# Weight halves of the plain products placed 64 bytes further on in SBUF, modulo 256

## The chip, the cores and the metric

The kernel runs on one core of a Trainium2 chip. The metric is the device time of one execution in microseconds, the median of several runs; lower is better. Beside it stands one profiled execution, from which all rows of the profile come.

## The reference

One transformer block over 512 tokens of width 1024, in fp32: a gated feed-forward, a mixer of two kinds of attention, a second gated feed-forward, and a last norm.

```python
def swiglu(h, w_gate, w_up, w_down):
    return (jax.nn.silu(h @ w_gate) * (h @ w_up)) @ w_down        # D_FF = 2816

    x = x + 0.5 * swiglu(rmsnorm(x, norm_ffn1), w_ffn1_gate, w_ffn1_up, w_ffn1_down)
    x = x + hybrid_mixer(rmsnorm(x, norm_mix), w_in, ..., w_out, rel_bias)
    x = x + 0.5 * swiglu(rmsnorm(x, norm_ffn2), w_ffn2_gate, w_ffn2_up, w_ffn2_down)
    return rmsnorm(x, norm_final)
```

The mixer projects h with w_in (2840 columns), runs eight heads of block attention and eight heads of compressed, selected and windowed attention with shared keys and values, and projects the result with w_out (1024 by 1024).

## The kernel before

Activations lie transposed: 128 features on the partitions, 512 tokens along the free dimension. TensorE (PE) multiplies a stationary operand, which a weight load (PEld in the profile) brings into the array, by a moving operand that streams through it. Each fp32 factor is kept as two fp32r halves, a rounded one (hi) and the rest (lo). `mm3` forms a product as three matmuls: hi by hi (L101), hi by lo (L102), lo by hi (L103). The loads of the next matmul's weights run beside the matmul before it.

There are two kinds of weight halves, each made by ScalarE (hi, a copy with rounding) and VectorE or, in parts of the mixer, GpSimd (lo, a subtraction) from a chunk that a DMA from SyncE's queue has brought:

- `whi`, `wlo`, from the pool `wp` (five buffers each), made by `halves` (L92, L94, L96). They serve the plain gate and up products (`pgu`; the first four of 22 blocks of 128 hidden features in each feed-forward, and there alone), the way down (`pd`, moving operand `h`), and in the mixer the projections (`pp`), the value projections (`pv`, where whi and wlo are the moving operand and `xo` the stationary one), the compression (`pc`) and the output projection (`pw<-o` and `pw<-kvn`). With `pd` of the last two hidden blocks of the second feed-forward, too, whi and wlo move.
- `sph`, `spl`, from the pool `sp` of each feed-forward (L236, L237). They serve the gate and up products of the other 18 hidden blocks, which `Ffn.pair` forms two blocks at a time by a scheme of seven products of half the size (256 columns): `pu`, `pv`, `pw` from moving operands `xo` (B11 and the like) and `th`, `tl` (sums of blocks). These are called two-block products below. (The mixer has tiles of the names pv and pw of its own; their moving operand tells them apart: two-block `pv` and `pw` have `sph` or `spl` as the weights.)

The order is written out by hand. In each feed-forward `lay` makes a list of steps: a plain stage (four hidden blocks of gate and up, then their way down, whose matmuls follow one another), then two-block steps, between which `mixed` and `between` lay the way down of the four hidden blocks before: each such triple of matmuls (one `mm3` of `pd`, 512 columns) stands alone or with another between groups of two-block products of 256 columns. `go` calls loads, sums and halves a fixed number of steps ahead. In the mixer `run` mixes projection matmuls into the attention steps.

A pool lays its tiles out in the order in which their names are first asked for, and the pools follow one another. The program holds two tiles that nothing uses, and that only move what follows: `gap` (64 bytes, in `sp` behind th and tl) and `rest` (192 bytes, in `cp`). The first bytes of the operands of TensorE, along a partition, as the program before places them:

| tile | role on TensorE | first address | modulo 256 |
|---|---|---|---|
| xo | moving; stationary for the mixer's pv | 28448 | 32 |
| raw (chunks from the DMA) | none | 61216 | 32 |
| whi | stationary; moving for the mixer's pv | 77600 | 32 |
| wlo | the same | 87840 | 32 |
| h | moving; stationary for the last pd | 108320 | 32 |
| th, tl (feed-forward) | moving | 141088, 153376 | 32 |
| sph, spl | stationary | 165728, 178016 | 96 |
| kvn, o, ak (mixer) | moving or stationary | 119072, 162592, 183072 | 32 |

Buffers of one name are 2048 bytes apart, and the slices that a matmul reads begin at multiples of 512 bytes in them, so the column holds for all of them.

Of the kernel before, what the change touches and what calls it, by code (L numbers as in the profile page):

```python
# [9 lines left out]
F32 = mybir.dt.float32  # L10
# [19 lines left out]
def block_kernel(ctx: ExitStack, tc: tile.TileContext, A: dict, out: bass.AP):  # L30
# [11 lines left out]
    wp = ctx.enter_context(tc.tile_pool(name="wp", bufs=2))  # L42
# [12 lines left out]
    def f32(ap):  # L55
        return ap.bitcast(F32)
# [16 lines left out]
    def load(src):  # L73
        v = chunk(src.shape[1:])
        nc.sync.dma_start(v, src)
        return halves(v)

    side = [False]
    last_hi = [None]

    def halves(src):

        n, width = src.shape[1:]
        per = S // width
        out = []
        for k in range(0, n, per):
            m = min(per, n - k)
            hi, lo = [
                wp.tile([128, S], F32R, name=name, tag=name, bufs=bufs)[:, :m * width].rearrange(
                    "p (a b) -> p a b", a=m) for name, bufs in (("whi", 5), ("wlo", 5))]  # L90
            v = src[:, k:k + m]
            last_hi[0] = nc.scalar.activation(hi, v, AF.Copy)  # L92
            if side[0]:
                nc.gpsimd.tensor_tensor(lo, v, f32(hi), ALU.subtract)  # L94
            else:
                nc.vector.tensor_tensor(lo, v, f32(hi), ALU.subtract)  # L96
            out += [(hi[:, i], lo[:, i]) for i in range(m)]
        return out
# [93 lines left out]
    class Ffn:  # L192
# [79 lines left out]
        def plain(self, f):  # L272
# [10 lines left out]
            def halves_of(m):  # L283
                with tc.issue_after(self.x_made.ins) if self.x_made and m else nullcontext():
                    got[m] = halves(got[m])
                if self.x_made and m:
                    self.x_made, self.first_up = None, last_hi[0]
# [104 lines left out]
        def down(self, w, fs, then, tags=("mm",), groups=(1,) * NK, kept_back=True, left=None):  # L392
# [10 lines left out]
            def halves_of(d):  # L403
                if d % (4 // n) == 0:
                    i = d * n % 8
                    with self.behind_lo() if kept_back else nullcontext():
                        parts = halves(raw[d * n // 8][:, i:i + 4])
                    for k, v in enumerate(parts):
                        got[d + k // n, k % n] = v
# [856 lines left out]
```

## Time and profile before

| | us |
|---|---|
| median of 3 runs (lowest to highest) | 983.82 (983.59 to 984.43) |
| the profiled execution: its time / its span | 983.34 / 981.5 |
| TensorE matmul busy | 969.0 |
| TensorE weight loads busy | 866.1 |
| VectorE busy | 779.9 |
| ScalarE busy | 563.6 |
| GpSimd busy | 135.4 |

The span goes from the first to the last instruction; 1.8 us of the execution's time lie around it. Busy time of TensorE counts overlapping matmuls once, and the ends of matmuls are modelled; how fast they follow one another is read from their starts in the timeline. A row of the timeline has the start and the duration in us, the engine, the line, the operation, the tiles (out<-moving,stationary for a matmul), the shape and the count. A row of the groups has the count, the busy time in us and the mean ns of one, then the engine's idle time before them and what ended it. A row of the waits has who waited for whom, us in total, times, and the longest. Some matmul records are missing from the trace; a missing one leaves a gap of its length between the starts.

### The profile page before, as it was taken

Reading aid. Unit: us, or ns where it says so; the run is one execution under the profiler, and the core shown is the slowest. Engines: PE = TensorE matmul, PEld = TensorE weight load, DVE = VectorE, ACT = ScalarE, POOL = GpSimd, SP = SyncE. Lnnn points to the kernel's source line nnn. Section 1 sums busy time; section 2 is a strip of 40 time slices with the busy share of each in tenths; the row PEclk is TensorE's granted clock in tenths of the full one; section 3 lists DMA queues with packets and bytes.
Section 4 is the critical chain, followed back from the end, with each engine's and each line's share of the span. In section 5 each row is a group of like instructions: output and inputs, shape, how many; then the busy total and the mean of one; then the engine's idle time right before and its main releaser. Section 6 shows DMA issues by size and latency. Waiting matters only on the chain.

```text
span 981.5 us, 17081 instructions
## 1 busy us (share of the span) xinstructions
PE 969.0 (99%) x6180; PEld 866.1 (88%) x6180; DVE 779.9 (79%) x1579; ACT 563.6 (57%) x1171; POOL 135.4 (14%) x180
## 2 busy tenths in 40 slices
PE   9999999999999999999999999999999999999996
PEld 7789999999999889889888888888999999999985
DVE  6897997787777488868788998889798778777744
ACT  6463664454554266677776787655466445554435
POOL 0000000000000000055666577100000000000002
PEclk9999999999999999999999999999999999999999
DMA  7355534332412125641311332135254323241102
GB/s 250 95 197 160 210 132 134 92 108 74 130 49 62 56 69 152 193 143 39 91 50 49 93 92 71 65 100 201 84 171 133 130 65 100 95 129 44 55 12 86
DMA packets 51592, 104.52 MB, mean 106 GB/s; under 512 B 10129, under 2 KB 16738, under 8 KB 51508
## 3 DMA queue, kind: packets, MB, share of 16 engines
q1 hardware_dynamic: 51220, 102.91, 33.2%
q8 instruction: 48, 0.79, 0.3%
q10 hardware_dynamic: 288, 0.52, 0.1%
q14 instruction: 36, 0.29, 0.1%
HBM read 97.98 MB, written 5.30 MB: 105 GB/s over the span
## 4 chain that ended last, share of the span: by engine, by line
PE 95%; ACT 2%; DVE 1%; issue 1%; DMA 0%; POOL 0%; POOLq 0%; ACTq 0%; DVEq 0%
PE pd L102 8%; PE pd L103 8%; PE pd L101 8%; PE pu L101 7%; PE pu L102 7%; PE pu L103 7%; PE pw L101 5%; PE pw L103 5%; PE pw L102 5%; PE pgu L101 3%; PE pgu L102 3%; PE pgu L103 3%; PE pp L101 3%; PE pp L103 3%; PE pv L103 3%; PE pv L101 3%
## 5 line engine op out<-in xcount | busy, mean ns | idle before, releaser
L236 ACT ACTIVATE sph<-aw 128x512 fp32r<-128x512 f32 x252 | 157.2, 630 | 197.7 <-PE pu L102 69.7
L237 DVE TENSOR_TENSOR spl<-aw,sph 128x512 fp32r<-128x512 f32 x252 | 172.3, 690 | 61.0 <-ACT sph L236 58.7
L92 ACT ACTIVATE whi<-raw 128x512 fp32r<-128x512 f32 (+2 forms) x202 | 122.2, 615 | 118.4 <-PE pd L102 44.2
L102 PE MATMUL pd<-h,whi 128*128 128x512 f32 x336 | 132.9, 395 | 0.0
L103 PE MATMUL pd<-h,wlo 128*128 128x512 f32 x336 | 131.3, 393 | 0.0
L101 PE MATMUL pd<-h,whi 128*128 128x512 f32 x336 | 130.6, 395 | 0.0
L96 DVE TENSOR_TENSOR wlo<-raw,whi 128x512 fp32r<-128x512 f32 (+1 forms) x166 | 109.7, 670 | 21.2 <-ACT whi L92 17.6
L101 PE MATMUL pu<-th,sph 128*128 128x256 f32 x432 | 119.8, 277 | 0.3 <-ACT wc L346 0.3
L103 PE MATMUL pu<-th,spl 128*128 128x256 f32 x432 | 119.7, 277 | 0.0
L102 PE MATMUL pu<-tl,sph 128*128 128x256 f32 x432 | 119.5, 277 | 0.0
L322 DVE TENSOR_TENSOR aw<-aw 128x512 f32<-128x512 f32 x144 | 99.0, 689 | 0.0
L531 DVE SCALAR_TENSOR_TENSOR x<-pd,x 128x512 f32<-128x512 f32 x88 | 60.1, 689 | 33.3 <-PE pd L103 33.3
L101 PEld LDWEIGHTS pu<-th,sph 128*128 128x128 f32 x432 | 81.2, 188 | 4.8 <-ACT wc L346 0.7
L102 PEld LDWEIGHTS pu<-tl,sph 128*128 128x128 f32 x432 | 81.2, 188 | 3.9
L103 PEld LDWEIGHTS pu<-th,spl 128*128 128x128 f32 x432 | 81.1, 188 | 0.1
L101 PE MATMUL pw<-xo,sph 128*128 128x256 f32 x288 | 79.9, 278 | 0.0
L102 PE MATMUL pw<-xo,sph 128*128 128x256 f32 x288 | 79.7, 277 | 0.0
L103 PE MATMUL pw<-xo,spl 128*128 128x256 f32 x288 | 79.6, 277 | 0.0
L103 PEld LDWEIGHTS pd<-h,wlo 128*128 128x128 f32 x336 | 63.3, 188 | 13.8
L102 PEld LDWEIGHTS pd<-h,whi 128*128 128x128 f32 x336 | 63.1, 188 | 4.1 <-DVE h L269 0.2
L101 PEld LDWEIGHTS pd<-h,whi 128*128 128x128 f32 x336 | 63.1, 188 | 3.7
L102 PEld LDWEIGHTS pw<-xo,sph 128*128 128x128 f32 x288 | 54.2, 188 | 3.6
(244 smaller groups left out, 2494.3 us busy)
## 6 DMA issues: line engine op xcount, KB each, us to landing
aw<-in_wg SPq DMA_DIRECT2D x72, 256.0 KB, 2.9
aw<-in_wu SPq DMA_DIRECT2D x72, 256.0 KB, 4.2
raw<-in_wd1a SPq DMA_DIRECT2D x20, 512.0 KB, 4.1
raw<-in_wd2a SPq DMA_DIRECT2D x20, 512.0 KB, 4.9
raw<-in_w_a SPq DMA_DIRECT2D x16, 512.0 KB, 3.6
raw<-in_w SPq DMA_DIRECT2D x8, 512.0 KB, 4.0
raw<-in_w_o SPq DMA_DIRECT2D x8, 512.0 KB, 4.1
raw<-in_wg SPq DMA_DIRECT2D x7, 512.0 KB, 4.2
```

Source lines behind the costliest of these rows:

```text
L92: last_hi[0] = nc.scalar.activation(hi, v, AF.Copy)
L96: nc.vector.tensor_tensor(lo, v, f32(hi), ALU.subtract)
L101: nc.tensor.matmul(p, w[0], v[0], start=first, stop=False, skip_group_check=again)
L102: nc.tensor.matmul(p, w[0], v[1], start=False, stop=False, skip_group_check=again)
L103: return nc.tensor.matmul(p, w[1], v[0], start=False, stop=last, skip_group_check=again)
L236: nc.scalar.activation(hi, v, AF.Copy)
L237: self.last_lo = nc.vector.tensor_tensor(lo, v, f32(hi), ALU.subtract)
L322: nc.vector.tensor_tensor(to, x, y, op)
L531: nc.vector.scalar_tensor_tensor(xs[d], p, 0.5, xs[d], ALU.mult, ALU.add)
```

## The change

At the first call of `halves`, two tiles that nothing reads or writes are asked for in the pool `wp`: `wgap` of 64 bytes ahead of whi and wlo, and `wrest` of 192 bytes behind them.

```diff
         n, width = src.shape[1:]
         per = S // width
         out = []
+        if not last_hi[0]:
+            wp.tile([128, 16], F32, name="wgap", tag="wgap", bufs=1)
         for k in range(0, n, per):
             m = min(per, n - k)
             hi, lo = [
                 wp.tile([128, S], F32R, name=name, tag=name, bufs=bufs)[:, :m * width].rearrange(
                     "p (a b) -> p a b", a=m) for name, bufs in (("whi", 5), ("wlo", 5))]
+            if not last_hi[0]:
+                wp.tile([128, 48], F32, name="wrest", tag="wrest", bufs=1)
             v = src[:, k:k + m]
             last_hi[0] = nc.scalar.activation(hi, v, AF.Copy)
```

`last_hi[0]` is set in the first call, so the tiles are asked for once. The instructions of every engine and of every queue are the same, in the same order; only addresses differ:

| tile | before, modulo 256 | after, modulo 256 | moved by |
|---|---|---|---|
| everything ahead of whi (x, xo, raw, the constants) | | the same | 0 |
| whi, wlo | 32 | 96 | 64 |
| everything behind (t, h, th, tl, sph, spl, aw, and the mixer's kvn, o, ak, aq, lp) | 32, or 96 for sph, spl, aw, wc | the same | 256 |

## The prediction

> **What bounds the kernel now.** I read first the page (span, busy shares, chain, costliest groups), then the waits, then TensorE's timeline.
>
> ```profile
> span 981.5 us, 17081 instructions
> ...
> PE 969.0 (99%) x6180; PEld 866.1 (88%) x6180; DVE 779.9 (79%) x1579; ACT 563.6 (57%) x1171; POOL 135.4 (14%) x180
> ...
> PEclk9999999999999999999999999999999999999999
> ...
> PE 95%; ACT 2%; DVE 1%; issue 1%; DMA 0%; POOL 0%; POOLq 0%; ACTq 0%; DVEq 0%
> ...
> L102 PE MATMUL pd<-h,whi 128*128 128x512 f32 x336 | 132.9, 395 | 0.0
> L103 PE MATMUL pd<-h,wlo 128*128 128x512 f32 x336 | 131.3, 393 | 0.0
> ...
> L101 PE MATMUL pu<-th,sph 128*128 128x256 f32 x432 | 119.8, 277 | 0.3 <-ACT wc L346 0.3
> ...
> L101 PE MATMUL pw<-xo,sph 128*128 128x256 f32 x288 | 79.9, 278 | 0.0
> ```
>
> TensorE (PE) is busy 99% of the span at full granted clock, and the chain that ended last is 95% matmuls. Who waits for whom:
>
> ```profile
> ACT sph L236 <- PE pu L102: 69.7, 64, 4.5
> ...
> ACT whi L92 <- PE pd L102: 44.2, 33, 3.7
> ...
> PE ps_t L959 <- DVE tl L964: 2.1, 3, 0.8
> ```
>
> ScalarE waits for TensorE; TensorE's own longest wait, summed, is 2.1 us. So the matmuls' spacing sets the end. The durations in the groups overlap (395 ns is longer than the spacing), so I use start-to-start times from the timeline.
>
> **The spacing is not the same everywhere, for the same shape.** First the down products of the plain stage, which follow one another (TensorE's timeline; first and last of 28 rows):
>
> ```profile
> 60.01 0.39 PE L101 MATMUL pd<-h,whi 128*128 128x512 f32 x1
> ...
> 66.13 0.39 PE L103 MATMUL pd<-h,wlo 128*128 128x512 f32 x1
> ```
>
> 27 steps in 6.12 us: 226.7 ns each. The same products laid between two-block products of 256 columns:
>
> ```profile
> 303.85 0.28 PE L103 MATMUL pv<-xo,spl 128*128 128x256 f32 x1
> 303.96 0.40 PE L101 MATMUL pd<-h,whi 128*128 128x512 f32 x1
> 304.20 0.40 PE L102 MATMUL pd<-h,whi 128*128 128x512 f32 x1
> 304.43 0.40 PE L103 MATMUL pd<-h,wlo 128*128 128x512 f32 x1
> 304.67 0.28 PE L101 MATMUL pv<-xo,sph 128*128 128x256 f32 x1
> ...
> 324.67 0.40 PE L101 MATMUL pd<-h,whi 128*128 128x512 f32 x1
> ...
> 332.94 0.40 PE L101 MATMUL pd<-h,whi 128*128 128x512 f32 x1
> ```
>
> Between the last two rows lie six equal rounds of three down products and six two-block products: 8.27 us, 1.378 us a round. At 226.7 ns and half of that (113.3 ns) a round would take 3 x 226.7 + 6 x 113.3 = 1.360 us. Each triple thus loses 18 ns, and the 303.96 to 304.67 rows put the loss in the triple (0.71 us for 0.68 us). Next the two-block products, in two stretches:
>
> ```profile
> 124.03 0.28 PE L103 MATMUL pu<-xo,spl 128*128 128x256 f32 x1
> ...
> 125.39 0.28 PE L103 MATMUL pw<-xo,spl 128*128 128x256 f32 x1
> ...
> 694.66 0.39 PE L102 MATMUL pd<-h,whi 128*128 128x512 f32 x1
> 694.88 0.39 PE L103 MATMUL pd<-h,wlo 128*128 128x512 f32 x1
> 695.11 0.28 PE L101 MATMUL pw<-xo,sph 128*128 128x256 f32 x1
> ...
> 696.41 0.28 PE L101 MATMUL pu<-xo,sph 128*128 128x256 f32 x1
> ```
>
> 12 steps in 1.36 us (113.3 ns) and 11 steps in 1.30 us (118 ns): the same kind of product has two states, and each holds over these whole rows. Last, the mixer's value products, where a weight half is the moving operand (first and last of 35 rows):
>
> ```profile
> 376.84 0.28 PE L103 MATMUL pv<-whi,xo 128*128 128x256 f32 x1
> ...
> 380.92 0.28 PE L101 MATMUL pv<-whi,xo 128*128 128x256 f32 x1
> ```
>
> 34 steps in 4.08 us: 120.0 ns. Beside these spacings I set the addresses that the program gives. Two-block halves sph/spl stand 64 bytes (modulo 256) from their moving operands xo, th, tl: 113 or 118 ns. In the value products both operands stand at the same place: 120 ns. In the triples both also stand at the same place, and there the loss begins with the first load of a whi that runs beside a product whose moving operand has its place. I read this as two streams out of SBUF, the moving operand of one product and the weights of the next, that get in each other's way when they run in step; 64 bytes apart they can miss one another.
>
> [...]
>
> **The change, part by part.** No instruction is added, removed or moved on any queue, and no wait; only places change. whi and wlo go from 32 to 96 modulo 256; everything behind them moves by 256 bytes.
>
> (a) Triples between two-block products. The page has 336 triples of pd; by the code 32 of each feed-forward block follow one another in its plain stage and 16 at the end of the first block, and some 16 kept-back ones run in a row at the ends of the two-block stages: 336 - 64 - 16 - 16 = 240 remain. After the change a load of whi beside xo, and beside h, stands 64 bytes off, as sph beside xo does in the 113.3 ns stretch. In such a product of 512 columns the load (whose own pace of 113 ns the two-block stretch shows) is over in the first half, and that half looks like the product of 256 columns in the 113.3 ns stretch; so I take 226.7 ns. Gain 240 x 18 ns = 4.3 us, all on the path, as TensorE has no wait there. Bounds: a gain of 4.3, or nothing; a loss is rival 2.
>
> (b) Products already at 226.7 ns: plain gate and up products, mixer's projections and output products. Their counts:
>
> ```profile
> L101 PE MATMUL pp<-xo,whi 128*128 128x512 f32 x128 | 52.3, 408 | 0.0
> L101 PE MATMUL pgu<-xo,whi 128*128 128x512 f32 x128 | 50.6, 397 | 0.0
> L101 PE MATMUL pv<-whi,xo 128*128 128x256 f32 x64 | 18.7, 296 | 0.0
> L101 PE MATMUL pw<-o,whi 128*128 128x512 f32 x32 | 13.3, 416 | 0.0
> L103 PE MATMUL pv<-whi,xo 128*128 128x280 f32 x32 | 8.9, 291 | 0.0
> ```
>
> With three products to a row (and a second row of 32 for the other output products) these are 3 x (128 + 128 + 64) = 960 of 512 columns. One place shows such a product with the load behind it 64 bytes off and no trouble before it: 694.88, whose next load is sph; it took 695.11 - 694.88 = 0.23 us, like its neighbours. So 0; bounds by the ends of (a) and rival 2.
>
> (c) Value products: 3 x (64 + 32) = 288 with whi/wlo moving. Now the weights xo stand 64 bytes behind the moving operand, not ahead, which no row shows. If that serves as well, 120.0 goes to 113.3: 288 x 6.7 ns = 1.9 us; if not, 0. I take the middle, 1.0 us, since 118 ns lies between. The mixer's steps lie beside waits on other engines, so some may come back as idle time.
>
> (d) Two-block products: place against xo unchanged modulo 256. But so far every distance is 0 or 64 also modulo 512; now sph from xo, and whi from h, stand 320 apart modulo 512. No row shows whether that counts. Only equal places show a loss in every stretch, and 320 is no more equal than 64, so 0; the bound is 118 instead of 113.3 ns on the products whose moving operand is xo, 3 x (288 + 144 + 144) = 1728, +8.1 us (their rows stand here and under rival 1).
>
> (e) The engines that write the halves, by shape:
>
> ```profile
> L236 ACT ACTIVATE sph<-aw 128x512 fp32r<-128x512 f32 x252 | 157.2, 630 | 197.7 <-PE pu L102 69.7 <-issue 60.5 <-PE pw L102 37.3
> L92 ACT ACTIVATE whi<-raw 128x512 fp32r<-128x512 f32 x192 | 118.1, 626 | 115.5 <-PE pd L102 44.2 <-PE pgu L102 26.3 <-PE pp L102 9.1
> ```
>
> At 96 (sph) 630 ns, at 32 (whi) 626 ns. 4 ns x 192 would be 0.8 us of ScalarE, which waits for TensorE far longer; 0.
>
> Sum: -4.3 - 1.0 = -5.3 us. The profiled execution took 983.34 us (span 981.5 and 1.8 around it), so 978.0; the median of the runs shown, 983.82, is 0.48 above it, so I forecast 978.5.
>
> **The rivals.**
> 1. The 118 ns state takes over (slower). A two-block stretch in that state stays in it; in the trace the stretches come back to 113 ns after a stall or behind a triple, and I take it that today's triple, with its extra 18 ns, shifts the two streams. If a triple no longer shifts them, the state could last to the next stall. Two-block products number 3 x (432 + 288 + 144 + 144) = 3024, the last two groups as in:
>
> ```profile
> L101 PE MATMUL pu<-xo,sph 128*128 128x256 f32 x144 | 40.1, 279 | 0.2 <-ACT t L368 0.2
> L101 PE MATMUL pv<-xo,sph 128*128 128x256 f32 x144 | 39.8, 278 | 0.0
> ```
>
> All of them at 118 instead of 113.3 would be +14.2 us, less 5.3: +8.9, 992.7 at worst, 985.6 if one of the two blocks falls into it. It decides from a share of 5.3/14.2 = 37% more of the products. Against it: the same state must survive all the triples of a block in a row, and each gives the loads time to catch up. 12%.
> 2. A 512-column product at 64 bytes has a loss of its own. In the rounds above the third of the triple, whose next load is sph, takes 0.23 to 0.24 us, the first two 0.23 to 0.24 too; at 4 ns on each of 960 it is +3.8 us, and a triple would lose 12 instead of 18 ns, -1.4: +2.4 without (c), 986.2. The row at 694.88 speaks against it. 8%.
> 3. The place of the halves does not count: the loss in the triples comes from the switch between 256 and 512 columns. Then all stays: 983.8. For it: no whi was ever at another place. Against it: 120.0 and 113.3 ns, both of 256 columns, without any switch. 10%. [...]
>
> **How the numbers follow.** Forecast (a gain of 3 to 8.5 us) 70%: 975.3 to 980.8 around 978.5; the lower end adds to (a) all of (c) and 2 us for today's 118 ns stretches and restarts. With rival 3 the range reaches 984.0 and holds 80%. A measurement of this kernel tells 0.2%, 2 us, from nothing. Faster 0.71, same 0.10, slower 0.19 (rivals 1 and 2, less a little).
>
> **What would show it.** Right: the rounds of 1.378 us read 1.36; the means of pd fall from 395 to about 390, as in the plain stage; whole two-block stages end some 2 us earlier each; the value products at 113 to 118 ns. Wrong: rounds of 1.378 us as now (rival 3); two-block products at 118 ns through a whole stage, their mean above 279 (rival 1); pgu and pp spaced wider than 226.7 ns (rival 2).

## The result and the profile after

| | before | after |
|---|---|---|
| median of 5 runs each, us (lowest to highest) | 983.59 (982.05 to 984.43) | 992.70 (991.71 to 993.91) |
| the profiled execution: its time / its span, us | 983.34 / 981.5 | 993.91 / 992.1 |

The kernel after takes 1.010 times as long (95% interval 1.0087 to 1.0112): 9.1 us slower, where 5.3 us less was forecast. The profiled execution of after lies 1.2 us above its median, so the two spans differ by 10.6 us. The change adds four lines ahead of all that is named here: L105 to L107 of after are L101 to L103 of before, L96 is L92, L240 is L236. First the page of after:

```profile
span 992.1 us, 17081 instructions
...
PE 978.2 (99%) x6180; PEld 871.1 (88%) x6180; DVE 780.5 (79%) x1579; ACT 563.4 (57%) x1171; POOL 135.4 (14%) x180
...
PE 87%; DVE 4%; ACT 4%; issue 2%; DMA 1%; POOL 0%; ACTq 0%; POOLq 0%; DVEq 0%
```

As many instructions; TensorE is still busy 99%, and its busy time grew by 9.2 us. VectorE, ScalarE and GpSimd are as busy as before within 0.6 us. The chain that ended last holds less of TensorE (87% against 95%); whether TensorE waits more is read from the waits:

```profile
ACT sph L240 <- PE pu L106: 72.6, 64, 4.6
...
ACT whi L96 <- PE pd L106: 46.0, 35, 3.8
...
PE ps_t L963 <- DVE tl L968: 2.0, 3, 0.7
```

It doesn't: its longest wait is 2.0 us in all (2.1 before), and ScalarE waits somewhat longer for it. So the 10 us are again in the spacing of the matmuls. The groups (by shape) show it dimly, since durations overlap (pgu's mean is 400 ns, its starts lie 233.3 apart):

```profile
L105 PE MATMUL pu<-th,sph 128*128 128x256 f32 x432 | 120.6, 279 | 0.5 <-ACT wc L350 0.5
L105 PE MATMUL pw<-xo,sph 128*128 128x256 f32 x288 | 80.5, 280 | 0.3 <-ACT sph L240 0.2
...
L105 PE MATMUL pp<-xo,whi 128*128 128x512 f32 x128 | 52.7, 411 | 0.2 <-ACT whi L96 0.2
L105 PE MATMUL pgu<-xo,whi 128*128 128x512 f32 x128 | 50.8, 400 | 0.0
```

A two-block product's mean went from 277 to 279 ns (pu) and 278 to 280 (pw), pp from 408 to 411, pgu from 397 to 400: everything is wider by some 2 to 3 ns. The timeline tells where. Plain products in a row, gate and up first, then the way down (first and last of 28 each):

```profile
39.63 0.40 PE L107 MATMUL pgu<-xo,wlo 128*128 128x512 f32 x1
...
45.93 0.39 PE L107 MATMUL pgu<-xo,wlo 128*128 128x512 f32 x1
...
59.93 0.39 PE L105 MATMUL pd<-h,whi 128*128 128x512 f32 x1
...
66.23 0.40 PE L107 MATMUL pd<-h,wlo 128*128 128x512 f32 x1
```

27 steps in 6.30 us, 233.3 ns each, in both. Before, the same row of way down stood at 226.7, and so did the gate and up products (28 of them, 27 steps in 6.12 us):

```profile
39.61 0.39 PE L103 MATMUL pgu<-xo,wlo 128*128 128x512 f32 x1
...
45.73 0.39 PE L103 MATMUL pgu<-xo,wlo 128*128 128x512 f32 x1
```

Now the rounds of one triple and six two-block products, at the place where before had six equal rounds of 1.378 us:

```profile
327.78 0.28 PE L105 MATMUL pw<-xo,sph 128*128 128x256 f32 x1
...
328.49 0.39 PE L105 MATMUL pd<-h,whi 128*128 128x512 f32 x1
...
329.18 0.28 PE L105 MATMUL pw<-xo,sph 128*128 128x256 f32 x1
...
329.87 0.39 PE L105 MATMUL pd<-h,whi 128*128 128x512 f32 x1
...
330.56 0.28 PE L105 MATMUL pw<-xo,sph 128*128 128x256 f32 x1
...
331.27 0.39 PE L105 MATMUL pd<-h,whi 128*128 128x512 f32 x1
```

The triples take 0.69 us instead of 0.70 to 0.71. But the six two-block products take 0.71, 0.69 and 0.71 us: 118 ns each before one triple, 113.3 behind it (but for the first, of 119 in the trace's nanoseconds), 118 behind the next. Here a triple turns one state of the stretch into the other; before, each triple here left it at 113.3. Last, two-block products without triples (55 rows) and value products (41 rows):

```profile
723.77 0.28 PE L107 MATMUL pv<-xo,spl 128*128 128x256 f32 x1
...
729.89 0.28 PE L107 MATMUL pu<-xo,spl 128*128 128x256 f32 x1
```
```profile
381.21 0.28 PE L105 MATMUL pv<-whi,xo 128*128 128x256 f32 x1
...
385.92 0.28 PE L106 MATMUL pv<-wlo,xo 128*128 128x256 f32 x1
```

54 steps in 6.12 us are 113.3 ns: the pure two-block stretch is unharmed though sph now stands 320 from xo modulo 512. The value products take 4.71 us for 40 steps, 117.8 ns, against 120.0.

**Where the 10.6 us went.** I took every product's start-to-start time from the trace, less 226.7 ns (512 columns), 113.3 (256) or 124.0 (280), and summed what is above that; a gap over 16 ns (a wait, a switch to another shape) is counted apart. "Triples" are the 230 that stand between two-block products with no such gap in them; "value products" here include those of the compression (`pc`). Each loss, here and below, is that of one profiled execution. Two versions below keep every distance of before modulo 256 (the move alone, and the place without the distance): they give its losses again within 0.2 us, but up to 1.0 us more in the gaps, so the last column's difference shows nothing.

| loss, us | triples (690 products) | other 512-column (some 1,290) | two-block (some 3,010) | value products | gaps over 16 ns | 
|---|---|---|---|---|---|
| before | 4.60 | 2.75 | 1.64 | 1.61 | 17.82 |
| after | 3.49 | 8.35 | 6.89 | 1.41 | 18.77 |
| difference | -1.11 | +5.60 | +5.25 | -0.20 | +0.95 |

The sum is +10.5. Setting the two programs' matmuls against each other one by one, after is 0.9 us late at the end of the first plain stage (71 us), 3.9 at the end of the two-block stage (333 us), 5.9 at the end of the mixer (636 us), 7.2 behind the second plain stage (687 us), 10.3 at 939 us and 10.6 at the end: both parts are spread over the whole kernel.

### The profile page after: what moved, and what is told of

Same layout as the page of the kernel before. It is cut to its first block, busy times and chain, and to the rows that moved or that the text cites. A ratio compares the mean times of both kernels' runs of the same rounds, so it can differ in the third digit from the quotient of the medians.

```text
span 992.1 us, 17081 instructions
## 1 busy us (share of the span) xinstructions
PE 978.2 (99%) x6180; PEld 871.1 (88%) x6180; DVE 780.5 (79%) x1579; ACT 563.4 (57%) x1171; POOL 135.4 (14%) x180
## 4 chain that ended last, share of the span: by engine, by line
PE 87%; DVE 4%; ACT 4%; issue 2%; DMA 1%; POOL 0%; ACTq 0%; POOLq 0%; DVEq 0%
PE pd L106 8%; PE pd L107 8%; PE pd L105 8%; PE pu L105 6%; PE pu L107 6%; PE pu L106 6%; PE pw L105 5%; PE pw L107 5%; PE pw L106 5%; PE pgu L106 3%; PE pgu L107 3%; PE pgu L105 3%; PE pv L105 2%; PE pv L106 2%; PE pv L107 2%; PE ps_t L963 2%
## 5 line engine op out<-in xcount | busy, mean ns | idle before, releaser
L240 ACT ACTIVATE sph<-aw 128x512 fp32r<-128x512 f32 x252 | 157.3, 630 | 205.1 <-PE pu L106 72.6
L96 ACT ACTIVATE whi<-raw 128x512 fp32r<-128x512 f32 (+2 forms) x202 | 122.3, 615 | 123.7 <-PE pd L106 46.0
L107 PE MATMUL pd<-h,wlo 128*128 128x512 f32 x336 | 131.9, 395 | 0.0
L105 PE MATMUL pd<-h,whi 128*128 128x512 f32 x336 | 130.0, 393 | 0.0
L105 PE MATMUL pu<-th,sph 128*128 128x256 f32 x432 | 120.6, 279 | 0.5 <-ACT wc L350 0.5
L107 PE MATMUL pu<-th,spl 128*128 128x256 f32 x432 | 120.2, 278 | 0.0
L105 PEld LDWEIGHTS pu<-th,sph 128*128 128x128 f32 x432 | 81.2, 188 | 4.7 <-ACT wc L350 0.9
L107 PEld LDWEIGHTS pu<-th,spl 128*128 128x128 f32 x432 | 81.2, 188 | 0.1
L105 PE MATMUL pw<-xo,sph 128*128 128x256 f32 x288 | 80.5, 280 | 0.3 <-ACT sph L240 0.2
L107 PE MATMUL pw<-xo,spl 128*128 128x256 f32 x288 | 79.8, 278 | 0.0
L107 PEld LDWEIGHTS pd<-h,wlo 128*128 128x128 f32 x336 | 63.1, 188 | 13.6
L105 PEld LDWEIGHTS pd<-h,whi 128*128 128x128 f32 x336 | 63.2, 188 | 4.2
L105 PEld LDWEIGHTS pw<-xo,sph 128*128 128x128 f32 x288 | 54.1, 188 | 4.1 <-ACT sph L240 0.9
```

The source lines that it names most:

```text
L105: nc.tensor.matmul(p, w[0], v[0], start=first, stop=False, skip_group_check=again)
L107: return nc.tensor.matmul(p, w[1], v[0], start=False, stop=last, skip_group_check=again)
```

## The experiments

The letters in the expectations: P is the theory that the distance modulo 256 between a product's moving operand and the weights loaded beside it sets the spacing; M, that the move of everything behind by 256 bytes costs; W, that whi and wlo cost at any place but 32, by themselves. "Distance" below is always weights less moving operand, modulo 256. The loss in the tables is that of the last table. Each ratio is to the kernel before, run beside it.

**The move alone.** whi stays at 32, everything behind moves by 256:

```diff
-            wp.tile([128, 16], F32, name="wgap", tag="wgap", bufs=1)
...
-                wp.tile([128, 48], F32, name="wrest", tag="wrest", bufs=1)
+                wp.tile([128, 64], F32, name="wrest", tag="wrest", bufs=1)
```

> whi and wlo stay at 32 modulo 256, all behind them moves by 256 bytes as in the changed kernel (whi is now 256 from h modulo 512, sph 320 from xo). Theory P (only the distance modulo 256 of a loaded weight half from the moving operand beside it counts): as before, 982 to 985 us, plain products of 512 columns 226.7 ns apart, two-block products mostly 113.3 ns. Theory M (the 256-byte move, or the distance modulo 512, is what cost the 9 us): the two-block products at 118 ns in about half of their stretches, 988 to 993 us.

983.16 us against 982.63, ratio 1.0004 [0.9995, 1.0013]: nothing. M falls, and with it the fear of (d) that sph at 320 modulo 512 could matter.

**Other distances of whi and wlo.** The kernel after with other sizes of the two tiles: 32 and 32 (distance 128 from xo and h), 48 and 16 (192), 8 and 56 (32).

```diff
-            wp.tile([128, 16], F32, name="wgap", tag="wgap", bufs=1)
+            wp.tile([128, 32], F32, name="wgap", tag="wgap", bufs=1)
...
-                wp.tile([128, 48], F32, name="wrest", tag="wrest", bufs=1)
+                wp.tile([128, 32], F32, name="wrest", tag="wrest", bufs=1)
```

> whi and wlo at 160, so 128 from xo and h. Theory P: the spacing of plain products in a row depends on the distance; 128 is a new point. If places repeat every 128 bytes, it is as at distance 0: plain 226.7 ns, triples lose 18 to 20 ns, value products 120 ns, 982 to 985 us. If they repeat every 256, 128 may be as 64 (plain about 233 ns, 990 to 994 us) or free of loss everywhere (about 975 us). Theory M: as the changed kernel, 990 to 994 us, whatever the distance.

> whi and wlo at 224, so 192 from xo and h (64 the other way round). Theory P: if only the size of the distance counts, as the changed kernel, plain products about 233 ns apart and 990 to 994 us; the value products, where the moving operand and the weights change parts, then stand as the two-block products do (113 or 118 ns). If the sign counts, another time. Theory M: 990 to 994 us.

> whi and wlo at 64, so 32 from xo and h, which is half of the step of 64 bytes. Theory P with 64-byte lines: all operands so far begin at half a line (32 modulo 64); these begin at a line, and if lines matter the plain products change from both 226.7 and 233 ns. If only whole lines of distance count, as distance 0 or 64: 983 or 992 us. Theory M: 990 to 994 us.

| distance of whi | us | ratio [95%] | triples | other 512 | two-block | value |
|---|---|---|---|---|---|---|
| 0 (before) | 983.59 | | 4.60 | 2.75 | 1.64 | 1.61 |
| 32 | 989.31 | 1.0070 [1.0055, 1.0085] | 5.33 | 8.17 | 1.44 | 1.36 |
| 64 (after) | 992.70 | 1.0100 [1.0087, 1.0112] | 3.49 | 8.35 | 6.89 | 1.41 |
| 128 | 998.26 | 1.0162 [1.0147, 1.0177] | 4.41 | 7.24 | 13.05 | 1.73 |
| 192 | 990.38 | 1.0097 [1.0066, 1.0127] | 3.44 | 4.28 | 9.43 | 0.88 |

Of the four runs at 192 three took 988.9 to 990.7 us and one 995.6; its losses are those of the shortest, 988.87. Each of these four distances makes the plain rows wider than the 226.7 ns of distance 0; 128, the farthest of them modulo 256, is hardly better than 64 (232.2 against 233.3 ns). The way down in a row at 128, 192 and 32 (first and last of 28 products each, 27 rows):

```profile
56.62 0.40 PE L107 MATMUL pd<-h,wlo 128*128 128x512 f32 x1
...
62.89 0.40 PE L107 MATMUL pd<-h,wlo 128*128 128x512 f32 x1
```
```profile
56.77 0.39 PE L107 MATMUL pd<-h,wlo 128*128 128x512 f32 x1
...
62.95 0.39 PE L107 MATMUL pd<-h,wlo 128*128 128x512 f32 x1
```
```profile
56.66 0.40 PE L105 MATMUL pd<-h,whi 128*128 128x512 f32 x1
...
62.96 0.40 PE L105 MATMUL pd<-h,whi 128*128 128x512 f32 x1
```

232.2, 228.9 and 233.3 ns. Whether there are lines of 64 bytes, as the expectation for 32 supposes, no run shows. The two-block loss is a second effect: its own distance is 64 in all five, yet it lies between 1.4 and 13 us, as the triples leave the stretch in one state or the other. With whi at 192 the second block stays at 117.7 ns even where no triple stands (52 steps in 6.12 us; after has 113.3 at the same place):

```profile
723.83 0.28 PE L106 MATMUL pw<-xo,sph 128*128 128x256 f32 x1
...
729.95 0.28 PE L105 MATMUL pw<-xo,sph 128*128 128x256 f32 x1
```

And with whi at 192 the value products, whose moving operand is whi, have their weights xo at 64:

```profile
376.73 0.28 PE L105 MATMUL pv<-whi,xo 128*128 128x256 f32 x1
...
381.38 0.28 PE L107 MATMUL pv<-whi,xo 128*128 128x256 f32 x1
```

41 steps in 4.65 us, 113.4 ns: the same shape that takes 120.0 at 0 and 117.8 at 192. So for 256 columns 64 can be good (113.4 ns) and 0 is bad (120.0), as the prediction read it; for 512 columns in a row it is the other way round (233.3 and 226.7).

**Other distances of sph and spl.** The kernel before, with its `gap` tile of 16 floats made 32, 48 and 8:

```diff
-            sp.tile([128, 16], F32, name="gap", tag="gap", bufs=1)
+            sp.tile([128, 32], F32, name="gap", tag="gap", bufs=1)
```

> The kernel before with sph and spl (the halves of the two-block products) at 160 instead of 96, so 128 from xo and th, and whi and wlo as before. Theory P (the distance of the next load from the moving operand sets the spacing): plain and mixer products as before, 226.7 ns in a row; the two-block products at a new distance. e2 showed value products at 128 at 5.8 ns over 113.3, so some 119 ns in the two-block stretches: 3024 x 4 to 6 ns more, 994 to 1001 us. Theory W (the loss comes from whi and wlo being away from 32, whatever the distance): as before, 981 to 985 us.

> sph and spl at 224, so 192 from xo and th; whi and wlo as before. Theory P: plain products as before; value products at 192 in the changed kernel lay 4.3 ns over 113.3, so two-block products near 118 ns: 3024 x 4 ns, about 994 us; if they have a 113.3 ns state that goes with the state in which plain products at distance 0 run clean, the triples' loss goes and it ends at 976 to 979 us. Theory W: as before, 981 to 985 us.

> sph and spl at 64, so 32 from xo and th; whi and wlo as before. Theory P: plain products as before; value products at 224 (32 the other way) in e4 lay 3.7 ns over 113.3, and products of 256 columns ahead of a whi at 32 there 3.4: two-block products at 117 ns, 3024 x 3.5 ns, 992 us or a little more. Theory W: as before, 981 to 985 us.

| distance of sph | us | ratio [95%] | triples | other 512 | two-block |
|---|---|---|---|---|---|
| 128 | 998.14 | 1.0160 [1.0144, 1.0177] | 3.91 | 2.53 | 18.76 |
| 192 | 992.15 | 1.0093 [1.0078, 1.0108] | 3.25 | 2.57 | 12.80 |
| 32 | 995.78 | 1.0129 [1.0114, 1.0144] | 4.89 | 2.70 | 15.05 |

The plain rows (distance 0, untouched) keep their 226.7 ns (2.53 to 2.70 us lost by the other 512-column products, 2.75 before); only the two-block products lose, 4 to 6 ns each. So the plain rows follow the place of whi and wlo alone, and the two-block products lose with the place of sph and spl even where whi and wlo stand still. That speaks for P, and against any account by the amount of memory or by the other engines.

**h at whi's new place.** The kernel after with two more unused tiles, so that h too stands at 96: distance 0 from h to whi, 64 from xo to whi, 0 from h to sph.

```diff
+            hp.tile([128, 16], F32, name="hgap", tag="hgap", bufs=1)
+            sp.tile([128, 48], F32, name="hrest", tag="hrest", bufs=1)
             self.th, self.tl = [sp.tile([128, 4, 3, HT], F32R, name=n, tag=n, bufs=1) for n in ("th3", "tl3")]
```

> The changed kernel (whi, wlo at 96) with h moved to 96 too, all behind it in place modulo 256: distance 0 from h to whi and wlo again, 64 from xo, and h to sph 0. Theory P: the way down of the plain stage returns to 226.7 ns, while the plain gate and up products and the mixer's projections stay at 233 ns; that is some 240 x 6.4 ns = 1.5 us less than the changed kernel, about 991 us if the two-block stretches keep their state, less if the triples leave them clean. Theory W (whi away from 32 costs by itself): the way down stays at 233 ns and the time at 992 to 994 us.

993.28 us, 1.0104 [1.0089, 1.0119]. The plain way down is back at 227.1 ns (24 steps in 5.45 us), gate, up and the mixer's products stay 6.6 ns wide: W falls. A round of it:

```profile
309.45 0.39 PE L105 MATMUL pd<-h,whi 128*128 128x512 f32 x1
309.68 0.39 PE L106 MATMUL pd<-h,whi 128*128 128x512 f32 x1
309.90 0.39 PE L107 MATMUL pd<-h,wlo 128*128 128x512 f32 x1
310.13 0.28 PE L105 MATMUL pw<-xo,sph 128*128 128x256 f32 x1
...
310.84 0.39 PE L105 MATMUL pd<-h,whi 128*128 128x512 f32 x1
```

The triple loses nothing (0.68 us; in the trace's nanoseconds 146 of the 230 lose less than 0.5, the other 84 lose 15 to 23). Yet the round is longer than before's 1.38 us: 1.39, because the six two-block products behind the triple stay at 118 ns (0.71 us). All triples lose 1.71 us instead of 4.60, the two-block products 12.2 instead of 1.64.

**The place without the distance.** The kernel before with one small tile ahead of everything 64 bytes longer; all places move together, whi to 96 as in after.

```diff
-    cp.tile([128, 48], F32, name="rest")
+    cp.tile([128, 64], F32, name="rest")
```

> The kernel before with everything behind its first small tables, the moving operands xo, th, tl, h, o among them, moved by 64 bytes: whi and wlo come to 96 modulo 256, as in the kernel after, and sph and spl to 160, but every distance between weights and moving operand stays as in the kernel before. If the distance modulo 256 is what counts: no change, 983 us within 0.2%, plain products at 226.7 ns, triples losing some 20 ns. If the place of whi and wlo itself counts (96 worse than 32): slower by up to the 9 us of the kernel after, plain gate and up products at 233 ns.

982.63 us, 0.9995 [0.9985, 1.0004], and each loss as before within 0.2 us (4.60, 2.57, 1.52, 1.62). The place itself counts for nothing; P stands.

**h alone.** The kernel before with `hgap` and `hrest` of 16 and 48, 32 and 32, 48 and 16 floats, so that only the way down's distances change:

> The kernel before with only h (the moving operand of the way down) moved by 64 bytes, so that whi stands 192 from h, and sph 0 from h; whi stands 0 from xo and sph 64 from xo as before. If the distance counts: gate and up products and the mixer's as before; the plain way down wider by some 2.5 ns a product (the figure that distance 192 gave), 0.5 us in all. Triples lose less than today's 20 ns, some 5 to 10; if it is the triple's loss that brings the two-block stretches back to 113.3 ns, these now keep 118 ns over many rounds: 984 to 990 us. If the two-block stretches' state has nothing to do with the triple's loss, they stay at 113.3 ns and the time falls to some 980 us.

> As before with h alone moved by 128 bytes: whi 128 from h, sph 192 from h. If the distance counts: way down in a row wider by 5.7 ns, 1.1 us in all; triples lose some 15 ns instead of 20 (gain 1 us), and the two-block stretches come back to 113.3 ns behind some triples only: 984 to 989 us. If the stretches' state does not hang on the triple's loss: 983 us.

> As before with h alone moved by 192 bytes: whi 64 from h as in the kernel after, sph 128 from h, all else as before. If the distance counts: way down in a row at 233 ns (1.2 us in all), gate and up products and the mixer's at 226.7 ns; the triples' loss between 13 ns (the kernel after) and 20 ns, and the two-block stretches alternate between 113.3 and 118 ns as in the kernel after if it is below 18: 984 to 989 us. What the kernel after pays beyond this time is then what its xo products pay.

| h to whi / h to sph | us | ratio [95%] | triples | other 512 | two-block |
|---|---|---|---|---|---|
| 192 / 0 | 986.12 | 1.0036 [1.0023, 1.0049] | 1.94 | 3.18 | 6.30 |
| 128 / 192 | 985.69 | 1.0031 [1.0017, 1.0045] | 3.79 | 4.11 | 3.89 |
| 64 / 128 | 984.90 | 1.0020 [1.0009, 1.0032] | 1.99 | 4.30 | 3.57 |

The way down goes to 228.9, 233.7 and 233.3 ns in a row (27 steps in 6.18, 6.31 and 6.30 us; 128 gave 232.2 above); gate and up stay at 226.7 to 227.0. The triples' loss falls by up to 2.7 us, and comes back in the two-block products. At 64 / 128 the rounds are no shorter than before's, though its triple loses only 9 ns:

```profile
328.79 0.39 PE L101 MATMUL pd<-h,whi 128*128 128x512 f32 x1
...
329.47 0.28 PE L101 MATMUL pu<-th,sph 128*128 128x256 f32 x1
329.60 0.28 PE L102 MATMUL pu<-tl,sph 128*128 128x256 f32 x1
...
330.17 0.39 PE L101 MATMUL pd<-h,whi 128*128 128x512 f32 x1
```

1.38 us: 0.68 us for the triple, and the rest of the loss stands behind it (0.13 us from the first two-block product to the second, where 0.113 would do; in the trace's nanoseconds the first three take 122, 115 and 115). In none of the fourteen placements does the median round come below 1.380 us. That left open what the triples' loss of 20 ns belongs to: the distance, or the turn from 256 to 512 columns and back.

**Fewer turns.** The kernel before, all places as there, with the triples between two-block products taken two, or four, at a time (here the lines for four; the line that sets `self.turn` to 0 at the start is left out):

```diff
-                self.between(self.held == 0)
+                self.turn += self.held == 0
+                self.between(4 * (self.held == 0 and self.turn % 4 == 0))
```

> The kernel before, all places as there, with the kept-back triples laid two at a time between two-block products at every second place (90 groups of six products and 52 of three, where before has 230 of three). If the 20 ns that before loses at a triple are the price of one turn from 256 to 512 columns and back, whatever the place of the weights: about 88 turns fewer, 88 x 20 ns = 1.8 us less, 981.6 us. If they are the price of each 512-column product whose load has the same place modulo 256: as many products, no change, 983.3 us. A wait for weights or for a bank of PSUM, which groups could bring, would show in the waits.

> As the run before it, with four triples at every fourth place (39 groups of twelve, 39 of three, some 30 of other sizes; about 110 turns where before has some 240). Price of a turn: 130 x 20 ns = 2.6 us less, 980.7 us. Price of each product: 983.3 us. The longest two-block row without triples also grows to four times its length, so scalar and vector work gets due in bunches: if that makes TensorE wait, the time rises above 983 us.

| triples at a time | us | ratio [95%] | all 512-column products | two-block |
|---|---|---|---|---|
| one (before) | 983.17 | | 7.35 | 1.64 |
| two | 989.53 | 1.0065 [1.0051, 1.0079] | 6.04 | 9.59 |
| four | 989.39 | 1.0068 [1.0055, 1.0081] | 4.94 | 9.97 |

Both slower, and yet the 512-column products lose 1.3 and 2.4 us less, where a price by the turn gave 1.8 and 2.6 and a price by the product 0. At these places, then, the loss is paid behind the turn and not by every product at distance 0. With two at a time TensorE waits no more than before; with four, one wait for sph of 0.9 us is new, a small part of the 7.5 us by which its profiled execution is longer. What neither expectation had is the row behind a group. Four triples and the two-block products behind them:

```profile
772.62 0.40 PE L101 MATMUL pd<-h,whi 128*128 128x512 f32 x1
...
775.37 0.28 PE L101 MATMUL pv<-xo,sph 128*128 128x256 f32 x1
...
779.61 0.28 PE L101 MATMUL pu<-th,sph 128*128 128x256 f32 x1
```

The twelve take 2.75 us, some 30 ns above 12 x 226.7, where four triples lost 80. But the next 36 products take 4.24 us, 117.8 ns each. In the trace's nanoseconds a row of six or of twelve at distance 0 loses some 6, 9, 2, 6 and 4 ns and then nothing (26 ns in all), and leaves the two-block products at 118 ns (behind 88 of 90 rows of six, and all 36 of twelve); a lone triple loses 6, 9 and 5 and leaves them at 113.3, also where they stood at 118 before it.

No version here beats the kernel before.

## Why the prediction was wrong

**(a) Triples, -4.3 us: the step failed.** They gained 1.11 us, 15.2 instead of 20.0 ns a triple. The sum put the loss down to equal places, paid by each product. The runs with fewer turns show that at these places it is paid once behind the turn: twelve products in a row at the same distance 0 lose 26 ns, not 80; and with h at 96, where whi again has the place of h, most triples lose nothing. Rival 3 named "the switch between 256 and 512 columns", and this half of it holds for before; its condition, that the place does not count, fell with its forecast, as a triple lost anything from 0 (most of them, h at 96) to 23 ns (whi at 32) by placement. The step also took 226.7 ns at 64 from the argument that a 512-column product's first half looks like a 256-column one. That the load is over in the first half was an estimate from the 113 ns pace, which no row shows: a load of pd and one of pu take 188 ns each in the trace of before. And what 256 columns do at 64 (113.3 ns in the settled row) did not tell what 512 do there (233.3).

**(b) Plain rows, 0: the larger failure, +5.60 us.** The evidence was one row, 694.88, the last product of a row that had settled at distance 0, with the two-block weights loading beside it. That product costs nothing in the trace of before (226 ns); but in a row at 64 the products lose 9 and 4 ns in turn, or 6 to 7 each. One clean product at the edge of a row is not a row, and in the triples of before the third product, with the same load behind it, lost 4.8 ns on average. This is rival 2. The loss that it named is there (233.3 against 226.7 ns in a row at 64), and its size was too small: 4 ns on 960 products against 4.4 ns more (6.5 less today's 2.1) on some 1,290, since the way down in rows (some 315 products), which part (b) left out, counts too.

**(c) Value products, -1.0 us.** -0.20 was measured. In settled rows 192 gives 117.8 ns where 64 gave 113.4, so the guess between the two ends was not far off for a row. But 96 of the 288 products have 280 columns, to which the sum gave the 6.7 ns of a 256-column row that it had not seen for them: in the trace they lose 0.34 us before and 0.36 after.

**(d) The 320 modulo 512, and (e) the writers: 0, as forecast.** The move alone changed nothing beyond 0.13%; by the page, ScalarE's 202 writes of whi take 122.2 us before and 122.3 after, 615 ns each in both.

**Rival 1: half true.** +5.25 us on the two-block products, where all of them at 118 ns would have been +14.2. Its condition, a triple that no longer sets the stretch back, was met: the triple of before sets the stretch back to 113.3 ns, and in after one often does not. But the size of the triple's loss alone does not decide it, as the rival held. Triples of 20 ns (before) and 23 (whi at 32) leave 113.3 ns; in after, of the 216 with at least three two-block products on either side, 96 of 12 or 13 ns turned 113.3 into 118, 90 of 15 or 16 ns turned it back, and 30 of 20 to 23 ns found it at 118 and left it so; those of 0 (h at 96) leave it as it was. Against it stood that the 118 ns state must survive every triple of a block; it need not, it is enough that most triples turn the state over. The time it gave at worst, 992.7, is the time measured, but by chance: half of the loss is rival 2's, which the sum of rival 1 held at none.

## What to carry to other kernels

When TensorE is busy all the time (99% of the span here), take the spacing of matmuls from their starts, by shape and by neighbours; a few ns on thousands of products are the whole of the result. Where a kernel's rows settle into a good spacing, the turn that seems to waste time may be what resets the next row (here a triple that lost 20 ns left six products at 113.3 ns, and twelve products that lost 26 ns left 36 at 117.8): price an edit to it together with the row behind it, over a whole round. And test a place by moving everything together once, and each operand alone: here the run that moved all told distance from place, and those that moved one operand told whose distance it was.

## What was not expected of the hardware

- The matmuls' spacing followed the distance between the moving operand and the weights: whi and wlo moved alone by 64 bytes changed it (226.7 to 233.3 ns in a row of 512 columns); all operands moved together (ratio 0.9995), or all behind whi and wlo by 256 bytes (1.0004), did not. Of the distances that were run, the best differs by length. In a row of 512 columns: 226.7 ns at 0, 233.3 at 32 and at 64, 232.2 to 233.7 at 128, 228.9 at 192. Of 256 columns: 120.0 at 0; 113.3 or 117.7 at 64; 117.8 at 192; in two-block rows of some 50 products 118.3 at 32, 118.7 at 128 and 117.7 at 192. In a row a product's own weights have the same place as the next ones, so the rows do not tell which of the two counts; and sph at distance 0 from xo was not run, so the 120.0 is that of the value products alone.
- At 64 the 256-column row has two states, and each lasted through rows of 50 products and more; what went before bears on which one it is (with triples taken four at a time, 118 ns behind all 36 rows of twelve, 113.3 behind 38 of 39 lone triples). Why the states exist, and why the distance counts and a move by 256 bytes does not, no run here shows: the trace has starts, not reads of memory. The two streams that get in each other's way were the prediction's reading.
- What a turn between the lengths costs is not fixed. At before's places a row of three 512-column products loses 20 ns and one of six or twelve 26; elsewhere a triple lost from 0 (most of them, h at 96) to 23 (whi at 32). Yet no placement has a median round below 1.380 us, before's own, 20 ns above the sum of the best spacings.
